# Sixteen weight units: VectorE makes all low parts of the projections' weights, GpSimd none

## The chip, the cores and the metric

One Trainium2 chip, one core. The metric is device time in microseconds (us) of one execution. TensorE ran at its full granted clock (1.00) in the profiled execution.

## What is computed

One layer of a streaming encoder over 576 tokens (512 of a prompt, 64 new ones with a cache of 128 rows), in float32. In short:

```
h   = x @ W_in                       # columns: k, q, v of two head groups, an index part, forget gates
mix = concat(ForgettingAttention(h_A),      # 8 heads: scores + decay, causal mask, softmax, @ V
             IndexedSparseAttention(h_B))   # 8 heads: rope, only the top-k rows by an index score
x   = LN1(alpha * x + mix @ W_o)
x   = LN2(alpha * x + relu(x @ W_up)^2 @ W_down)
x   = x + sigmoid(x @ W_g + b_g) * (p @ W_ple)
```

The top-k is 128 of up to 512 rows for the prompt, 48 of 192 for the sample. The part of the program that matters here is the projection to k, q and v and the attention that runs beside it.

## The kernel before, in words

Every large product is made in three passes of TensorE: a float32 operand is split into a high part and a low part (the rest), and high x high, high x low and low x high are summed. For a weight this takes three steps. A DMA on SP's queue brings the raw unit `wraw` (128 x 1024). ScalarE rounds it into the high half of `whl` (line 149, CAST). Then `raw - high` gives the low half (line 155, TENSOR_TENSOR). For the 24 units of the k, q and v projections each step is cut into two pieces of 128 x 512, so two high pieces and two low pieces per unit. Which engine makes the low pieces is the argument `eng` of `Weights.split`: VectorE (DVE), or GpSimd (POOL) when a unit was added with `pool_l`. In the kernel before, units 0 to 7 (k, q, v of head pairs 0 and 1, k and q of pair 2) have their low pieces on VectorE and units 8 to 23 (v of pair 2 up to v of pair 7) on GpSimd. The output projection's units and all later ones are on VectorE.

`WT.step()` is called after every six matmuls and emits one piece if its data have been asked for long enough ago and a `whl` buffer is free. There are three `whl` and three `wraw` buffers in this part. Two units are thus prepared ahead of the one in use.

The projections are a loop over head pairs p = 0 to 7. In it `drive(proj(p + 1), 24, ticks(9), 27)` interleaves the 24 steps of the next pair's three projections with 27 steps of the attention of pair p. A pair has nine attention jobs (4 query blocks x 2 heads for the prompt, one for the sample). A job goes through the engines in a row of stages:

- `qk` (TensorE, lines 890 to 900): scores into a PSUM buffer `S`;
- `addmax` (VectorE, line 908): adds the bias and finds the row maximum, `S` to `sP`;
- `exp` (ScalarE, line 913), then `norm`: a reciprocal (VectorE, line 918) and a multiply, on ScalarE for pairs 0 to 3 and for the sample (line 920), on VectorE for the others (line 922);
- `ptrans` (TensorE, line 56): transposes `sP` into a PSUM buffer `T`; `pevac` (line 953) copies it to `PT`;
- after the last job `pv` (TensorE, lines 966 to 975) multiplies by V, and `oevac` (lines 985, 986) splits the result.

`S`, `T` and `X` share three PSUM buffers, so a late `addmax` or `pevac` stops TensorE.

Beside it run, on VectorE, the top-k selection (`choice`, lines 708 and 710: eight maxima of a row, then eight replaced, 16 times per block; it ends in pair 4) and, for pairs 4 to 7, the rotary embedding of k and q (lines 788 to 797: ScalarE copies four pieces `xr`, VectorE does three passes over 128 x 576). GpSimd also makes the low part of k (`KLP`, lines 810 and 811, two of 64 x 512 for each of the pairs 2 to 7).

The order on each engine is the program's order as a scheduler lays it out when the kernel is built. Each engine then works through its own list in order and waits where an input is not there.

Of the kernel before, what the change touches and what calls it, by code (L numbers as in the profile page):

```python
# [36 lines left out]
def tile_hybrid_step(ctx: ExitStack, tc: tile.TileContext, I, O):  # L37
# [241 lines left out]
    WT = Weights()  # L279
# [94 lines left out]
    U = {}  # L374
    WT.ring(sbw, 3, 3, "a")
    qkv = I["w_qkv"]
    for p in range(8):
        for x, kind in enumerate("kqv"):
            U[kind, p] = WT.add(qkv[p * 3 + x], 128, pool_l=(p * 3 + x > 7))
    for j in range(8):  # L380
        U["o", j] = WT.add(I["w_o6"][j], 128)
    for k in (6, 7):
# [1463 lines left out]
```

## Time and profile before

| | |
|---|---|
| median of 3 runs | 765.42 us (765.17 to 766.64) |
| the profiled execution: its time, its span | 766.22 us, 764.5 us |
| TensorE matmuls busy | 751.9 us (98%) |
| VectorE busy | 571.8 us (75%), 1119 instructions |
| ScalarE busy | 472.8 us (62%) |
| GpSimd busy | 109.8 us (14%), 130 instructions |
| GpSimd on line 155 | 42.2 us, 32 instructions, from 78.2 to 228 us of the span |
| DMA | 101.35 MB, 133 GB/s in the mean |

Busy time of TensorE is counted up to the modelled end of each matmul, so 98% busy does not mean that it ran at its peak. The chain of waits is followed back from the last instruction; idle time of an engine that nothing waits for costs nothing. In the rows of the timeline the columns are: start, duration, engine, line, operation, output <- input, shape and count, and in brackets the idle time before it with what ended it.

### The profile page before, as it was taken

How to read it: one execution, taken by the hardware profiler on the slowest of the kernel's cores; microseconds unless marked ns; L12 is line 12 of the kernel's file. 1: busy time of each engine (PE TensorE's matmuls, PEld its weight loads, DVE VectorE, ACT ScalarE, POOL GpSimd, SP SyncE). 2: the span in 40 equal slices, each digit the busy share in tenths (PEclk: the TensorE clock that was granted, in tenths of full speed). 3: DMA queues.
4: the chain of work that ended last, by engine and by line, in shares of the span. 5: the costliest groups of instructions: out<-in, count | busy, mean ns of one | idle time of the engine just before them, and what ended most of it. 6: DMA issues, size and time to landing. Idle time of an engine off the chain costs nothing.

```text
span 764.5 us, 14624 instructions
## 1 busy us (share of the span) xinstructions
PE 751.9 (98%) x5679; PEld 731.5 (96%) x5679; DVE 571.8 (75%) x1119; ACT 472.8 (62%) x931; POOL 109.8 (14%) x130
## 2 busy tenths in 40 slices
PE   9999999999999999999999999999999999999997
PEld 7999988999899999999999999999999999999997
DVE  6788888888777865779777579866898666657643
ACT  6589777897676635788654577435764466625451
POOL 7100324344241000100000000000000000011000
PEclk9999999999999999999999999999999999999999
DMA  8438344244222315352546666667667664730001
GB/s 288 167 70 150 128 134 122 93 139 176 78 85 86 114 58 173 111 177 80 123 110 176 148 159 172 148 164 180 155 149 178 152 154 152 288 111 30 28 29 69
DMA packets 38197, 101.35 MB, mean 133 GB/s; under 512 B 6000, under 2 KB 10224, under 8 KB 38000
## 3 DMA queue, kind: packets, MB, share of 16 engines
q1 hardware_dynamic: 34384, 87.61, 37.1%
q0 software_dynamic: 3456, 12.58, 10.1%
q8 instruction: 44, 0.72, 0.4%
q10 hardware_dynamic: 288, 0.22, 0.1%
q14 instruction: 25, 0.20, 0.1%
HBM read 85.26 MB, written 9.54 MB: 124 GB/s over the span
## 4 chain that ended last, share of the span: by engine, by line
PE 80%; DVE 12%; ACT 6%; issue 2%; DVEq 0%; ACTq 0%
PE g L305 39%; PE m L305 15%; PE n L305 13%; PE g L293 2%; PE T L56 2%; PE V L975 2%; DVE dbias L710 2%; DVE whl L155 1%; ACT xr L788 1%; DVE m L708 1%; ACT whl L149 1%; PE m L469 1%; PE m L483 1%; PE S L900 1%; PE S L898 1%
## 5 line engine op out<-in xcount | busy, mean ns | idle before, releaser
L149 ACT CAST whl<-wraw 128x1024 fp32r<-128x1024 f32 (+2 forms) x190 | 154.9, 828 | 83.9 <-PE g L305 50.0
L155 DVE TENSOR_TENSOR whl<-wraw,whl 128x1024 fp32r<-128x1024 f32 (+2 forms) x158 | 157.8, 1008 | 53.4 <-ACT whl L149 52.8
L305 PE MATMUL m<-AH,whl 128*128 128x288 f32 x736 | 176.7, 307 | 0.0
L305 PE MATMUL g<-BH,whl 128*128 128x288 f32 (+2 forms) x680 | 143.3, 298 | 0.0
L305 PEld LDWEIGHTS m<-AH,whl 128*128 128x128 f32 x736 | 126.4, 188 | 1.7 <-issue 1.0
L305 PEld LDWEIGHTS g<-BH,whl 128*128 128x128 f32 x680 | 111.1, 188 | 1.3
L305 PE MATMUL m<-AL,whl 128*128 128x288 f32 x368 | 108.8, 296 | 0.0
L305 PE MATMUL g<-BL,whl 128*128 128x288 f32 (+2 forms) x340 | 100.6, 296 | 0.3 <-DVE BL L1250 0.3
L305 PEld LDWEIGHTS m<-AL,whl 128*128 128x128 f32 x368 | 69.5, 189 | 0.6
L305 PEld LDWEIGHTS g<-BL,whl 128*128 128x128 f32 x340 | 64.0, 188 | 0.9 <-DVE BL L1250 0.7
L210 POOL DMA_DIRECT2D wraw<-in_w_dram x24 | 20.8, 866 | 287.1 <-DMA wraw<-in_w_dram 207.5
L913 ACT ACTIVATE sP<-sP,st 128x128 f32<-128x128 f32 (+4 forms) x72 | 39.4, 549 | 35.4 <-DVE st L908 35.3
L155 POOL TENSOR_TENSOR whl<-wraw,whl 128x512 fp32r<-128x512 f32 x32 | 42.2, 1334 | 90.1 <-ACT whl L149 74.9
L305 PE MATMUL m<-BH,whl 128*128 128x288 f32 x192 | 43.0, 302 | 0.0
L305 PE MATMUL g<-s,whl 128*128 128x288 f32 x288 | 42.1, 295 | 0.0
L305 PE MATMUL n<-BH,whl 128*128 128x288 f32 x192 | 42.0, 294 | 0.0
L305 PEld LDWEIGHTS g<-s,whl 128*128 128x128 f32 x288 | 39.5, 188 | 0.0
L56 PE MATMUL T<-ident,sP 128*128 128x128 f32 (+1 forms) x176 | 31.3, 273 | 1.5 <-DVE sP L922 0.6
L305 PEld LDWEIGHTS m<-BH,whl 128*128 128x128 f32 x192 | 32.0, 188 | 0.5 <-issue 0.3
L305 PEld LDWEIGHTS n<-BH,whl 128*128 128x128 f32 x192 | 32.0, 188 | 0.0
L1520 ACT ACTIVATE g<-n 128x288 f32<-128x288 f32 x24 | 9.5, 395 | 35.6 <-PE n L305 35.6
L305 PE MATMUL m<-BL,whl 128*128 128x288 f32 x96 | 28.3, 294 | 0.0
(331 smaller groups left out, 1664.3 us busy)
## 6 DMA issues: line engine op xcount, KB each, us to landing
wraw<-in_w_dram SPq DMA_DIRECT2D x48, 512.0 KB, 4.0
wraw<-in_w_dram POOLq DMA_DIRECT2D x24, 512.0 KB, 5.8
wraw<-in_w_qkv_dram SPq DMA_DIRECT2D x23, 512.0 KB, 3.7
wraw<-in_w_dram SPq DMA_DIRECT2D x24, 256.0 KB, 4.3
wraw<-in_w_up_dram SPq DMA_DIRECT2D x8, 512.0 KB, 3.9
wraw<-in_w_down_dram SPq DMA_DIRECT2D x8, 512.0 KB, 4.1
wraw<-in_w_gate_dram SPq DMA_DIRECT2D x8, 512.0 KB, 4.2
wraw<-in_w_o_dram SPq DMA_DIRECT2D x8, 384.0 KB, 3.0
```

What stands on the lines that cost most here:

```text
L56: PE.transpose(out, in_, ident[:n, :n])
L149: ACT.copy(self.hv[u][:, 0, c], src["tile"][:, c])
L155: eng.tensor_tensor(t[:, 1, c], src["tile"][:, c], f(t[:, 0, c]), OP.subtract)
L210: POOL.dma_start(t[:, :n], it["acc"], accum_op=OP.add)
L293: PE.matmul(ps, W(w, k, slice(0, 128)), a[:, k, sl], start=(len(terms) == 2 and n == 0), stop=False)
L305: mm = PE.matmul(ps, W(w, kw, wc), a[:, ka, cols], start=(first and i == 0), stop=(last and i == n - 1), skip_group_check=more)
L469: PE.matmul(mk[:, h, :HW], w0(part, k), a[:, k, h * HW:(h + 1) * HW], start=(k == 0 and i == 0), stop=(k == 7 and i == 2))
L483: PE.matmul(acc[b][:n[b], :304], a[:, k, b * 128:b * 128 + n[b]], ixw(part, k), start=(k == 0 and i == 0), stop=(k == 7 and i == 2))
L710: tc.keep_in_program_order(DVE.match_replace(out=s, in_to_replace=m, in_values=s, imm_value=GONE))
L913: ACT.activation(j["P"], j["P"], AF.Exp, bias=j["st"][:, 0:1], scale=-1.0, accum_out=j["st"][:, 2:3])
L975: PE.matmul(ps[r, x * 256 + c.start:x * 256 + c.stop], P["vt"][:, kb, r], t[:, hh, kb, c], start=(kb == 0), stop=(kb == n - 1))
L1520: ACT.mul(P.e, P.o, -1.0)
```

## The change

The argument `pool_l` is dropped for the 24 units, so `Weights.split` gets VectorE for all of them.

```diff
     for p in range(8):
         for x, kind in enumerate("kqv"):
-            U[kind, p] = WT.add(qkv[p * 3 + x], 128, pool_l=(p * 3 + x > 7))
+            U[kind, p] = WT.add(qkv[p * 3 + x], 128)
```

32 instructions of 128 x 512 leave GpSimd's list and stand in VectorE's. The scheduler lays out VectorE's list anew around them; ScalarE's changes at some places with it, and TensorE's at one (three matmuls of a projection move ahead of two transposes).

The first place is on VectorE in the attention of pair 2, where the top-k selection of block 2 (`dbias2`) runs beside the additions for the softmax (`sP_...<-S_...,causal`). Before:

```order
L708 MAX m8_118<-dbias2_111 128x8
L710 MATCH_REPLACE dbias2_111<-m8_118,dbias2_111 128x384
L708 MAX m8_118<-dbias2_111 128x8
L908 ISA sP_1625,st_1626<-S_1604,causal_113 128x128
L908 ISA st_1626 128x1
L710 MATCH_REPLACE dbias2_111<-m8_118,dbias2_111 128x384
L918 RECIPROCAL st_1586<-st_1586 128x1
L708 MAX m8_118<-dbias2_111 128x8
L918 RECIPROCAL st_1626<-st_1626 128x1
L710 MATCH_REPLACE dbias2_111<-m8_118,dbias2_111 128x384
```

In the changed kernel, from the same MAX on:

```order
L708 MAX m8_118<-dbias2_111 128x8
L155 TENSOR_TENSOR whl_1600<-wraw_1241,whl_1600 128x512
L710 MATCH_REPLACE dbias2_111<-m8_118,dbias2_111 128x384
L908 ISA sP_1625,st_1626<-S_1604,causal_113 128x128
L908 ISA st_1626 128x1
L708 MAX m8_118<-dbias2_111 128x8
L918 RECIPROCAL st_1586<-st_1586 128x1
L155 TENSOR_TENSOR whl_1600<-wraw_1241,whl_1600 128x512
L710 MATCH_REPLACE dbias2_111<-m8_118,dbias2_111 128x384
L918 RECIPROCAL st_1626<-st_1626 128x1
```

The two low pieces of a unit stand between the steps of the selection, and the selection's steps have moved back against the softmax: the MATCH_REPLACE and MAX behind the first MAX are now behind it by a softmax addition. A little further, before the first addition of 128 x 256 columns of this pair, 11 MAX and 11 MATCH_REPLACE of `dbias2` stood, and 11 and 10 stand now.

The second place is on VectorE in pair 3, where q of pair 4 is rotated (lines 789 to 791) while the jobs `sP_2256` (384 columns) and `sP_2288` (the sample's, bias `biasS`) are at their softmax. Before:

```order
L908 ISA sP_2256,st_2257<-S_2238,causal_113 128x384
L908 ISA st_2257 128x1
L908 ISA sP_2288,st_2289<-S_2275,biasS_114 128x192
L908 ISA st_2289 128x1
L789 SCALAR_TENSOR_TENSOR x32_2244<-m_2103,cosT_105 128x576
L790 TENSOR_TENSOR xr_2245<-xr_2245,sinT_106 128x576
L918 RECIPROCAL st_2257<-st_2257 128x1
L791 TENSOR_TENSOR x32_2244<-x32_2244,xr_2245 128x576
L918 RECIPROCAL st_2289<-st_2289 128x1
L908 ISA sP_2331,st_2332<-S_2315,causal_113 128x512
```

In the changed kernel:

```order
L908 ISA sP_2256,st_2257<-S_2238,causal_113 128x384
L908 ISA st_2257 128x1
L155 TENSOR_TENSOR whl_2271<-wraw_1940,whl_2271 128x512
L789 SCALAR_TENSOR_TENSOR x32_2244<-m_2103,cosT_105 128x576
L790 TENSOR_TENSOR xr_2245<-xr_2245,sinT_106 128x576
L908 ISA sP_2288,st_2289<-S_2275,biasS_114 128x192
L908 ISA st_2289 128x1
L791 TENSOR_TENSOR x32_2244<-x32_2244,xr_2245 128x576
L918 RECIPROCAL st_2257<-st_2257 128x1
L155 TENSOR_TENSOR whl_2271<-wraw_1940,whl_2271 128x512
L908 ISA sP_2331,st_2332<-S_2315,causal_113 128x512
```

The sample's addition now stands behind the low piece and two of the three passes of the rotation, and its reciprocal (not shown, it follows lines 796, 797 and a MATCH_REPLACE) behind the next job's addition.

The third place is ScalarE's list at the same moment. Before:

```order
L913 ACTIVATE sP_2256,st_2257<-sP_2256,st_2257 128x384
L913 ACTIVATE sP_2288,st_2289<-sP_2288,st_2289 128x192
L920 ACTIVATE sP_2256<-sP_2256,st_2257 128x384
L953 COPY PT_2318<-T_2299 128x3x128
L794 CAST qE_2242<-x32_2244 64x576
L795 CAST qO_2243<-x32_2244 64x576
L799 COPY QS0_166<-x32_2244 64x64 x2
L920 ACTIVATE sP_2288<-sP_2288,st_2289 128x192
```

In the changed kernel:

```order
L913 ACTIVATE sP_2256,st_2257<-sP_2256,st_2257 128x384
L953 COPY PT_2318<-T_2299 128x3x128
L913 ACTIVATE sP_2288,st_2289<-sP_2288,st_2289 128x192
L794 CAST qE_2242<-x32_2244 64x576
L920 ACTIVATE sP_2256<-sP_2256,st_2257 128x384
L795 CAST qO_2243<-x32_2244 64x576
L799 COPY QS0_166<-x32_2244 64x64 x2
L913 ACTIVATE sP_2331,st_2332<-sP_2331,st_2332 128x512
L953 COPY PT_2318<-T_2343 128x3x128
L747 COPY v32_2360<-m_2246 128x576
L920 ACTIVATE sP_2288<-sP_2288,st_2289 128x192
```

Both multiplies of line 920, which release transposes on TensorE, have moved back: the one of 384 columns behind line 794, the sample's behind the next job's exponential, a copy and line 747. In pairs 4 and 5 the sample's addition and its multiply move in the same way.

## Prediction, made before the changed kernel ran

> **What bounds the kernel now.** First the page, then the stretch of the change, then who stops TensorE in it.
>
> ```profile
> span 764.5 us, 14624 instructions
> PE 751.9 (98%) x5679; PEld 731.5 (96%) x5679; DVE 571.8 (75%) x1119; ACT 472.8 (62%) x931; POOL 109.8 (14%) x130
> L155 POOL TENSOR_TENSOR whl<-wraw,whl 128x512 fp32r<-128x512 f32 x32 | 42.2, 1334 | 90.1 <-ACT whl L149 74.9
> ```
>
> TensorE is busy for all but 12.6 us of the span. So the time moves only as far as TensorE's waits move. The third row is what the change takes from GpSimd: 32 x 1.334 = 42.2 us, all between 78 and 228 us. GpSimd waits ahead of them (90.1 us), and TensorE waits for none of them. The stretch as a whole, with columns length, PE, PEld, DVE, ACT and POOL busy (instructions), TensorE clock, DMA share and GB/s:
>
> ```profile
> core 0: us, PE busy (x) PEld busy (x) DVE busy (x) ACT busy (x) POOL busy (x), PEclk, DMA share, GB/s
> 78.00:230.00 152.00, 148.50 (x1175) 140.53 (x1174) 125.31 (x376) 116.76 (x291) 58.07 (x46) 1.00 0.38 118
> ...
> 110.00:120.00 10.00, 8.98 (x75) 8.35 (x76) 9.72 (x36) 7.97 (x21) 3.93 (x4) 1.00 0.33 112
> ```
>
> VectorE is busy for 125.31 of 152 us (82%) and idle for 26.7. TensorE idles 3.5 us. The fullest ten microseconds of VectorE, 110 to 120, are also those in which TensorE idles most (1.02 us). The waits of TensorE from 60 to 265 us, in us, times and longest:
>
> ```profile
> PE X L966 <- DVE st L908: 0.9, 1, 0.9
> PE T L56 <- DVE sP L922: 0.6, 1, 0.6
> PE S L890 <- ACT cosT L676: 0.6, 1, 0.6
> PE S L898 <- DVE st L908: 0.3, 1, 0.3
> PE X L56 <- ACT v L747: 0.3, 1, 0.3
> PE T L56 <- ACT sinT L676: 0.2, 1, 0.2
> PE T L56 <- ACT sP L920: 0.2, 1, 0.2
> PE T L56 <- DVE st L908: 0.2, 1, 0.2
> PE X L56 <- DVE st L908: 0.2, 1, 0.2
> ```
>
> They are 3.5 us together. That caps what the change can gain. All wait for the softmax chain on VectorE and ScalarE or for a copy; none waits for a weight. The loss has no such cap: a late addition or reciprocal on VectorE stops TensorE directly.
>
> **What leaves, what comes.** The 42.2 us on GpSimd were on no path, so taking them away gains nothing by itself. The low piece on VectorE is shown where it is made there already:
>
> ```profile
> 71.34 0.69 DVE L155 TENSOR_TENSOR whl<-wraw,whl 128x512 fp32r<-128x512 f32 x1
> 71.95 0.75 DVE L774 SCALAR_TENSOR_TENSOR qs<-m,qs 128x576 fp32r<-128x576 f32 x1
> ```
>
> It takes 0.69 us, and the next instruction starts 0.61 us after it. 32 of them take 32 x 0.61 = 19.5 us of VectorE's time.
>
> Against this stands what GpSimd's pieces cost VectorE. Two of their 16 pairs, the passes that VectorE ran beside them, and the groups of one pass inside and behind the stretch:
>
> ```profile
> 98.13 2.52 POOL L155 TENSOR_TENSOR whl<-wraw,whl 128x512 fp32r<-128x512 f32 x2 [6.00 <-ACT whl L149]
> 99.55 1.32 DVE L683 SCALAR_TENSOR_TENSOR dbiasS<-cosT,iw,dbiasS 64x192 f32<-64x192 f32 x1
> ...
> 218.90 1.41 DVE L791 TENSOR_TENSOR x<-x,xr 128x576 f32<-128x576 f32 x1
> L790 DVE TENSOR_TENSOR xr<-xr,sinT 128x576 f32<-128x576 f32 x6 | 7.4, 1235 | 0.0
> L790 DVE TENSOR_TENSOR xr<-xr,sinT 128x576 f32<-128x576 f32 x2 | 1.5, 748 | 0.0
> ```
>
> The pass of line 790 takes 0.75 us behind 230 us, where GpSimd makes no low pieces, and 1.235 in the mean inside. The pass at 99.55 ends at 100.87, just behind GpSimd's pair (98.13 + 2.52 = 100.65), and took 1.32 us where its like takes 0.41 (the row at 102.00 below). Eight passes of VectorE, the first at 99.55 and the last at 218.90, sit in this way behind a low piece. Their surplus over the free price is 0.91, 1.10, 0.83, 0.91, 0.66, 0.63, 0.91 and 0.66, together 6.6 us. So VectorE gets 19.5 - 6.6 = 12.9 us more to do, against 26.7 us idle. It would be busy for about 138 of 152 us (91%).
>
> The Trainium skill's Perfetto Trace Analysis, section Optimizing Scalar/DVE Operations, speaks against the change: where VectorE is saturated, work may well be handed to ScalarE or even GpSimd. Read strictly, all 12.9 us would be path and the median 778.3. The same sentence adds that between these two engines it might not help, since they share a port, and the 6.6 us agree with that half.
>
> The low pieces themselves are not due soon. Two units are prepared ahead of the one in use, no wait for `whl` stands in the list above, and GpSimd took 1.334 us for a piece that VectorE makes in 0.69. So a piece may stand a few instructions later in a list and delays nothing. The DMA that refills `wraw` waits for the same piece and is covered by the same distance; SP's queue gets nothing new. GpSimd's pieces of k, which stood behind its low pieces, can only start earlier.
>
> **Stretch a, 98 to 120 us.**
>
> ```profile
> 102.00 0.41 DVE L683 SCALAR_TENSOR_TENSOR dbiasS<-sinT,iw,dbiasS 64x192 f32<-64x192 f32 x1 [0.80 <-ACT sinT L676]
> L710 DVE MATCH_REPLACE8 dbias<-m,dbias 128x384 f32<-128x384 f32 x16 | 8.7, 542 | 0.0
> 118.83 0.41 DVE L908 CUSTOM_DVE_ANT_0 sP<-S,causal 128x256 f32<-128x256 f32 x1
> 119.31 0.34 PE L966 MATMUL X<-PTs,Vc 128*64 128x64 f32 x4 [0.88 <-DVE st L908]
> ```
>
> From 102.00 VectorE works without a gap until the addition at 118.83, and TensorE waits 0.88 us for it. By the new order two low pieces come in ahead of that addition and one MATCH_REPLACE of 0.54 (0.62 with the loading of its values) goes behind it. A piece that stands between a MAX and the MATCH_REPLACE that needs it also covers about 0.1 us between them, so two cost about 1.0: +0.4. At the start the 0.91 of the pass at 99.55 goes; the pieces that replace it run mostly in the 0.9 us in which VectorE waited before 99.06. VectorE and ScalarE are then about 0.65 us earlier at 102.00, and TensorE's 0.2 us there goes. Net: **-0.25 us**.
>
> **Stretch b, 157 to 167 us**, where the order moves the sample's job most:
>
> ```profile
> 157.94 0.36 DVE L908 CUSTOM_DVE_ANT_0 sP<-S,biasS 128x192 f32<-128x192 f32 x1 [1.12 <-PE S L891]
> 159.67 0.76 DVE L789 SCALAR_TENSOR_TENSOR x<-m,cosT 128x576 f32<-128x576 f32 x1 [1.37 <-ACT xr L788]
> 161.28 1.58 DVE L791 TENSOR_TENSOR x<-x,xr 128x576 f32<-128x576 f32 x1
> 158.35 0.62 ACT L149 CAST whl<-wraw 128x512 fp32r<-128x512 f32 x1
> 161.07 0.45 ACT L913 ACTIVATE sP<-sP,st 128x192 f32<-128x192 f32 x1
> 161.50 0.61 ACT L920 ACTIVATE sP<-sP,st 128x384 f32<-128x384 f32 x1
> 162.89 0.67 ACT L794 CAST qE<-x 64x576 fp32r<-64x576 f32 x1 [0.41 <-DVE x L791]
> 164.81 0.45 ACT L920 ACTIVATE sP<-sP,st 128x192 f32<-128x192 f32 x1
> 166.23 0.64 ACT L747 COPY v<-m 128x576 f32<-128x576 f32 x1
> 162.55 0.49 PE L56 MATMUL T<-ident,sP 128*128 128x128 f32 x3
> 165.31 0.44 PE L56 MATMUL T<-ident,sP 128*128 128x128 f32 x2 [0.22 <-ACT sP L920]
> ```
>
> The first low piece waits for ScalarE's high one (158.35 + 0.62 = 158.97) and runs to 159.6, inside the 1.37 us before 159.67: hidden. But the sample's addition waits in the list behind it and behind lines 789 and 790, so it runs at 161.0 instead of 157.94. The pass of 791 follows without its 0.83 and ends at 162.1. ScalarE: exponential of the sample to 161.9, line 794 to 162.8, and only then the multiply of 384 columns, to 163.4. Its transposes stood at 162.55: TensorE waits 0.9. The sample's multiply now follows lines 795 (like 794, 0.67) and 799, an exponential, a copy and line 747. Before, 799 began at 164.2 (two of 0.67 behind 162.89) and line 747 ended at 166.87, with the sample's multiply (0.36 to the next start) among them: 2.3 us without it. So it ends near 163.4 + 0.67 + 2.3 + 0.4 = 166.75, or a little before where ScalarE waited among them; I take 166.65. Its transposes stood at 165.31, now 166.0 (0.9 later, without their 0.22): another 0.65. Sum: 0.9 + 0.65 - 0.22 = **+1.35 us**. TensorE being later, its next two waits for line 908 (0.2 and 0.3 us above) go: **-0.5**.
>
> **The rest.** From 177 to 186 us the last steps of the selection and the second piece press on the multiplies of 256 columns on VectorE: between nothing and 0.9 (the size of b's first wait), I take +0.3, since VectorE's 0.91 at line 790 goes there too. From 187 to 196 the waits of 0.6 and 0.2 us have the same form as b, but line 922 is on VectorE, and the 0.66 of line 791 goes while a piece of 0.61 comes: -0.35, half of them, as TensorE arrives later by then. In pair 5 (215 to 224 us) the same walk ends before TensorE needs the transposes: 0. Behind 230 us nothing changes. Sum: -0.25 + 1.35 - 0.5 + 0.3 - 0.35 = **+0.55 us**.
>
> The profiled execution (766.22 us, of which 1.72 lie around the span) stands 0.80 above the median. On the profile the sum gives 766.8, on the median 765.42 + 0.55 = **766.0 us**.
>
> **Rivals.** *VectorE's lists run full* (slower). If the 12.9 us are not spread into the idle time but meet the softmax chain in each of pairs 3, 4 and 5 as in b, two more b's come (+2.7), and the +0.3 becomes 0.9: 769.3. For it: 91% in the mean, and the ten microseconds from 110 already at 97%. Against it: the new order moves the selection, which nothing waits for before pair 4's last jobs, back behind the additions.
>
> *The waits go* (faster). The walks in b and behind it rest on tenths of a microsecond. If the 6.6 us of blocked passes is what holds the softmax chain, the waits for VectorE (0.9, 0.6, 0.3, 0.2, 0.2) go and b does not come: 765.4 - 2.2 = 763.2. It decides this if the multiply of 384 columns in b ends before 162.55. Against it: ScalarE's list there stands as shown.
>
> *The low pieces are themselves blocked by GpSimd's k pieces* (slower). These stay on GpSimd, and pair 7 shows the meeting:
>
> ```profile
> 237.79 0.54 DVE L155 TENSOR_TENSOR whl<-wraw,whl 128x384 fp32r<-128x384 f32 x1
> 238.24 1.38 DVE L922 TENSOR_SCALAR sP<-sP,st 128x256 f32<-128x256 f32 x1
> 237.99 1.49 POOL L810 TENSOR_TENSOR KLP<-x,kE 64x512 fp32r<-64x512 f32 x1 [9.95 <-PE m L305]
> ```
>
> The multiply of 256 columns waits about 1.0 us for line 810. A low piece in its place at pairs 2 to 6 could lose as much five times. In pair 7 TensorE did not wait; if two of the five meet the path, with b: 766.0 + 2.0 = 768.0.
>
> The Trainium skill's SBUF — State Buffer, section Who interferes with whom, calls the port that VectorE and GpSimd share an exclusive lock. The 1.38 us agree. By that rule alone the change would swap one lock for another.
>
> **How the numbers follow.** 0.2% (1.5 us) is about what a measurement of this kernel can tell from no change. Chances: my sum within 1.5 us of the median 0.58, lists run full 0.19, low pieces blocked 0.10, waits go 0.13. Same 0.58; slower 0.29; faster 0.13. The likeliest case alone spans 764.4 to 766.9. The range takes in most of the two slower cases and the edge of the faster one: 763.8 to 769.0.
>
> **What would show it.** Right: line 155 with 32 more on VectorE at about 0.69 us and none on GpSimd; lines 790 and 791 at 0.75 in the stretch; VectorE at 138 us there; a wait of `T L56` for `sP L920` in pair 3; TensorE's waits up by about half a microsecond. Wrong: additions of line 908 that start over 3 us behind their scores in several pairs, or low pieces well above 0.7 us.

## The result, and the profile after

The changed kernel takes 770.11 us (median; 770.08 to 770.39), the kernel before 765.46 beside it. The ratio is 1.006, 95% interval 1.0048 to 1.0073: slower by 4.65 us, and outside the predicted range of 763.8 to 769.0. The profiled execution took 770.1 us, its span 768.4.

The page of the changed kernel: busy time of the engines, and the group of line 155 on VectorE (before: 158 instructions, 157.8 us).

```profile
PE 752.0 (98%) x5679; PEld 730.5 (95%) x5679; DVE 586.2 (76%) x1151; ACT 473.5 (62%) x931; POOL 68.7 (9%) x98
L155 DVE TENSOR_TENSOR whl<-wraw,whl 128x1024 fp32r<-128x1024 f32 (+2 forms) x190 | 182.7, 970 | 58.0 <-ACT whl L149 57.2
```

TensorE does the same 752 us of work, so the loss is waiting. The stretch of the prediction (columns as there), and then three groups of VectorE from 60 to 230 us:

```profile
78.00:230.00 152.00, 145.44 (x1147) 136.91 (x1146) 137.47 (x403) 116.35 (x286) 16.61 (x14) 1.00 0.38 117
```

```profile
L155 DVE TENSOR_TENSOR whl<-wraw,whl 128x512 fp32r<-128x512 f32 x35 | 26.9, 772 | 4.9 <-ACT whl L149 4.8
L791 DVE TENSOR_TENSOR x<-x,xr 128x576 f32<-128x576 f32 x6 | 4.7, 776 | 0.0
L790 DVE TENSOR_TENSOR xr<-xr,sinT 128x576 f32<-128x576 f32 x6 | 4.5, 749 | 0.0
```

VectorE is busy for 137.47 us, as forecast (138), and lines 790 and 791 run nearly free (0.749 and 0.776 us). The same work now ends later, though: from 77.6 to 233.5 us, where it stands in this trace, VectorE is busy for 140.1 us. And a low piece takes 0.772 us in the mean instead of 0.69. TensorE's waits from 60 to 269 us:

```profile
PE T L56 <- ACT sP L920: 3.2, 5, 1.0
PE X L966 <- DVE st L908: 1.4, 1, 1.4
PE T L56 <- DVE sP L922: 1.0, 2, 0.6
PE S L890 <- ACT cosT L676: 0.6, 1, 0.6
PE X L56 <- ACT v L747: 0.3, 1, 0.3
```

They are 6.5 us instead of 3.5: the transposes of softmax rows (`T L56`) wait 4.2 us, before 0.8 for the same two lines.

Where the time went is seen best by matching TensorE's instructions of the two traces in their order and taking the difference of their start times. This table is worked out in that way from the two timelines (set to 0 at 70 us; places are times of before; us). It has a row for every kernel that is told of below. In the names, "changed" and "before" are the kernel that the edit starts from, "back" means on GpSimd again, "alone" means that only these units moved to VectorE, and "k pieces" are lines 810 and 811.

| at | 104 | 124 | 150 | 160 | 181 | 186 | 198 | 228 | 270 |
|---|---|---|---|---|---|---|---|---|---|
| changed | -0.38 | -0.49 | 0.11 | 0.56 | 1.55 | 2.62 | 3.18 | 3.62 | 3.62 |
| changed, small k pieces | -0.46 | -0.59 | -0.59 | -0.59 | -0.01 | -0.05 | -0.07 | 0.38 | -0.05 |
| changed, k units back | -0.47 | -0.58 | -0.58 | -0.58 | 0.14 | 0.11 | -0.20 | 0.26 | 0.23 |
| changed, unit 18 back | -0.36 | -0.47 | 0.13 | 0.59 | 1.57 | 1.54 | 1.24 | 1.68 | 1.69 |
| changed, q units back | -0.38 | -0.51 | 0.09 | 0.56 | 1.46 | 2.46 | 2.48 | 2.46 | 2.45 |
| changed, q pieces later | -0.36 | -0.48 | 0.11 | 0.58 | 1.48 | 2.56 | 1.98 | 1.68 | 1.66 |
| before, q units alone | 0.00 | 0.00 | -0.01 | -0.01 | 0.52 | 0.48 | 0.19 | 0.67 | 0.67 |
| before, k units alone | 0.35 | 0.34 | 0.61 | 0.61 | 0.61 | 2.44 | 2.46 | 2.43 | 2.41 |
| before, unit 18 alone | 0.01 | 0.00 | 0.00 | 0.00 | -0.01 | 1.84 | 1.85 | 1.85 | 1.86 |
| before, v units alone | -0.02 | 0.32 | 0.32 | 0.32 | 0.96 | 0.92 | 0.02 | 0.03 | 0.02 |
| before, v units and pair 7's k pieces | 0.00 | 0.33 | 0.33 | 0.34 | 0.99 | 0.96 | 0.07 | 0.09 | -0.32 |
| changed, all k pieces on VectorE | 0.17 | 0.05 | 1.23 | 2.30 | 2.13 | 1.88 | 1.74 | 2.17 | 1.75 |
| before, small k pieces | 0.00 | 0.01 | 0.01 | 0.00 | -0.35 | -0.39 | -0.35 | -0.39 | -0.82 |

In the row of the changed kernel 3.62 us are lost by 228 us, in jumps. The largest between two columns is 1.07 us, from 181 to 186. The rest of the spans' difference (3.9 us) lies at the two ends, and the profiled execution of before stood 0.76 above its median of 765.46. So about 1 us of the 4.65 by the medians is not located here.

That jump in the traces, first before (VectorE's pass of line 790 and its multiply, GpSimd's low piece of k, TensorE's transposes):

```profile
179.41 1.66 DVE L790 TENSOR_TENSOR xr<-xr,sinT 128x576 f32<-128x576 f32 x1
182.57 0.35 DVE L922 TENSOR_SCALAR sP<-sP,st 128x256 f32<-128x256 f32 x1
182.84 0.69 DVE L708 MAX8 m<-dbias 128x8 f32<-128x512 f32 x1
182.65 1.43 POOL L810 TENSOR_TENSOR KLP<-x,kE 64x512 fp32r<-64x512 f32 x1 [2.20 <-ACT kE L805]
183.52 0.38 PE L56 MATMUL T<-ident,sP 128*128 128x128 f32 x2
```

and then in the changed kernel:

```profile
182.12 0.68 DVE L710 MATCH_REPLACE8 dbias<-m,dbias 128x512 f32<-128x512 f32 x1
182.78 1.43 DVE L155 TENSOR_TENSOR whl<-wraw,whl 128x512 fp32r<-128x512 f32 x1
184.13 1.36 DVE L922 TENSOR_SCALAR sP<-sP,st 128x256 f32<-128x256 f32 x1
182.38 1.28 POOL L810 TENSOR_TENSOR KLP<-x,kE 64x512 fp32r<-64x512 f32 x1 [15.38 <-ACT kE L805]
183.73 1.62 POOL L811 TENSOR_TENSOR KLP<-x,kO 64x512 fp32r<-64x512 f32 x1
185.64 0.41 PE L56 MATMUL T<-ident,sP 128*128 128x128 f32 x2 [0.56 <-DVE sP L922]
```

Before, the multiply started 0.08 us ahead of line 810 and took 0.35. Now a low piece that starts inside line 810 takes 1.43 us, ending half a microsecond behind it, and the multiply behind it falls into line 811 and takes 1.36. Where 0.35 us stood on VectorE, 2.8 stand, and TensorE waits. Free, the two would take about 1.0 (0.69 and 0.35). The new order has also put a step of the selection (182.12) ahead of the multiply. A pass is called held here where it takes longer beside an instruction of GpSimd than the same pass without one. The theories for the experiments were: **K**, VectorE's passes are held by GpSimd's lines 810 and 811; **P**, the place of the q units' pieces ahead of the sample's softmax (the stretch b of the prediction); **L**, VectorE's load, so much for each piece.

### The profile page after: what moved, and what is told of

The parts are those of the page before. It is cut to its first block, busy times and chain, and to the rows that moved or that the text cites. A ratio compares the mean times of both kernels' runs of the same rounds, so it can differ in the third digit from the quotient of the medians.

```text
span 768.4 us, 14614 instructions
## 1 busy us (share of the span) xinstructions
PE 752.0 (98%) x5679; PEld 730.5 (95%) x5679; DVE 586.2 (76%) x1151; ACT 473.5 (62%) x931; POOL 68.7 (9%) x98
## 4 chain that ended last, share of the span: by engine, by line
PE 75%; DVE 15%; ACT 8%; issue 1%; DMA 1%; DVEq 0%; ACTq 0%
PE g L305 38%; PE n L305 13%; PE m L305 12%; DVE whl L155 3%; PE g L293 2%; ACT xr L788 2%; DVE dbias L710 2%; PE T L56 2%; DVE m L708 2%; ACT whl L149 1%; PE V L975 1%; DVE sP L908 1%; PE m L469 1%; PE m L483 1%; DVE dbias L683 1%
## 5 line engine op out<-in xcount | busy, mean ns | idle before, releaser
L155 DVE TENSOR_TENSOR whl<-wraw,whl 128x1024 fp32r<-128x1024 f32 (+2 forms) x190 | 182.7, 970 | 58.0 <-ACT whl L149 57.2
L56 PE MATMUL T<-ident,sP 128*128 128x128 f32 (+1 forms) x176 | 31.5, 275 | 4.5 <-ACT sP L920 3.2
L56 PEld LDWEIGHTS T<-ident,sP 128*128 128x128 f32 (+1 forms) x176 | 21.6, 138 | 7.1 <-ACT sP L920 4.4
```

The source lines that it names most:

```text
L56: PE.transpose(out, in_, ident[:n, :n])
L155: eng.tensor_tensor(t[:, 1, c], src["tile"][:, c], f(t[:, 0, c]), OP.subtract)
```

## The experiments

The kernel before was timed beside them and took 765.77 to 765.90 us, 0.3 to 0.4 more than beside the changed kernel, which was timed in the first session alone. So a difference from 770.11 us carries that much doubt, and the ratios are to the kernel before. Units are numbered k, q, v from pair 0 on, so 9, 12, 15, 18, 21 are k units, 10, 13, 16, 19, 22 q units.

**Three q units back on GpSimd.**

```diff
-            U[kind, p] = WT.add(qkv[p * 3 + x], 128)
+            U[kind, p] = WT.add(qkv[p * 3 + x], 128, pool_l=(p * 3 + x in (16, 19, 22)))
```

> As the changed kernel, but the six low pieces of the q units of pairs 5, 6 and 7 (units 16, 19, 22) are on GpSimd again; 26 pieces stay moved. Theory P (place): the loss sits where these three units' pieces stand, ahead of the sample's addition and the rotation of q; in the changed kernel TensorE waits there 1.04 + 0.72 (pair 3), 0.43 + 0.68 (pair 4) and 0.52 us (pair 5), 3.4 us together, so 770.1 falls to about 766.7. Theory L (load): VectorE has 19.5 us more to do and every piece costs the same share of the 4.65 us lost, 0.145 us; 26 pieces give 765.5 + 3.8 = 769.2. Theory K (lock): the loss comes from GpSimd's pieces of k (lines 810, 811), which hold up VectorE; they are untouched, so 770.

768.89 us, ratio 1.004 (1.0028 to 1.0053). Only 1.2 us came back; P is not the main cause. Near L's number, but in the table the loss comes in the same jumps as in the changed kernel up to 186 us, not evenly.

**Only these q units on VectorE.**

```diff
+            U[kind, p] = WT.add(qkv[p * 3 + x], 128, pool_l=(p * 3 + x > 7 and p * 3 + x not in (16, 19, 22)))
```

> As the kernel before, but the six low pieces of units 16, 19 and 22 alone are on VectorE. Theory P: nearly the whole loss, 765.5 + 3.4 = 768.9. Theory L: 6 of 32 pieces, 765.5 + 0.9 = 766.3. Theory K: almost nothing, 765.5, since the units whose pieces meet lines 810 and 811 are the others.

766.70 us, ratio 1.001 (1.0001 to 1.0019). The two waits of stretch b come with these three units alone, and a third in pair 5:

```profile
163.48 0.55 PE L56 MATMUL T<-ident,sP 128*128 128x128 f32 x3 [0.97 <-ACT sP L920]
166.79 0.44 PE L56 MATMUL T<-ident,sP 128*128 128x128 f32 x2 [0.71 <-ACT sP L920]
...
224.00 0.44 PE L56 MATMUL T<-ident,sP 128*128 128x128 f32 x2 [0.55 <-ACT sP L920]
```

P's waits are real, but 1.7 us of waiting in pair 3 costs 0.5 by 181 us, since TensorE, once late, waits less for what follows. The kernel loses 0.9 us in all by P (766.70 against 765.83).

**The q units' pieces held back behind the rotation** (all on VectorE). Their low pieces are due 8 steps after the high ones instead of 2, and are emitted behind the last pass of the rotation.

```diff
-                        lo_at[0] = clock[0] + 2
+                        lo_at[0] = clock[0] + (8 if u in (16, 19, 22) else 2)
...
+                    with tc.issue_after(rotated[0]) if u in (16, 19, 22) else ExitStack():
```

> All 32 pieces on VectorE as in the changed kernel, but the pieces of units 16, 19 and 22 are emitted six steps later and held in VectorE's list behind the last pass of the rotation of q (line 797 of the kernel before). The load on VectorE is the same, only the place of six pieces differs; the sample's addition and both multiplies of ScalarE are back in their old order. Theory P: 766.7 as in the experiment that gives these pieces back to GpSimd. Theory L and theory K: 770.

767.80 us, ratio 1.0027 (1.0017 to 1.0037). In pair 3 nothing was gained: the two waits became 0.61 us (for the copy to `PTs`) at 169 and 0.78 at 171, and the table has 1.48 at 181 us, like the 1.55 of the changed kernel. The gain lies in pairs 4 and 5: behind 186 us this row wins 0.9 where the changed kernel loses 1.0. There P had 1.63 of its 3.4 us; L and K had nothing.

**Small pieces of k.** Lines 810 and 811 of pairs 2 to 7 do 64 of their 512 columns (the rest of k's low parts is left out); the lists of the other engines stay as in the changed kernel.

```diff
-        q(lambda: eng.tensor_tensor(KL[lo, 0], k32[lo, :NP], f(QE[lo, :NP]), OP.subtract))
+        q(lambda n=64 if p > 1 else NP: eng.tensor_tensor(KL[lo, 0, :n], k32[lo, :n], f(QE[lo, :n]), OP.subtract))
...
```

> As the changed kernel, but GpSimd's pieces of k for pairs 2 to 7 (lines 810, 811) work on 64 of 512 columns, so most of the low part of k is left out for these pairs. The lists of VectorE, ScalarE and TensorE are the same as in the changed kernel, row for row; GpSimd holds VectorE up for about 0.3 us at a time and not 1.3. Theory K: TensorE's wait of 0.56 us for line 922 in pair 4 goes, and up to 1 us each at pairs 2, 3, 5: 768 to 769. Theories P and L: 770.

766.23 us, ratio 1.0006 (0.9997 to 1.0014): less than even K expected. All low pieces are on VectorE, each in its place in the list, and 3.9 of the 4.65 us are gone. The same pass and multiply as above:

```profile
180.71 0.67 DVE L155 TENSOR_TENSOR whl<-wraw,whl 128x512 fp32r<-128x512 f32 x1
181.30 0.41 DVE L922 TENSOR_SCALAR sP<-sP,st 128x256 f32<-128x256 f32 x1
180.31 0.31 POOL L810 TENSOR_TENSOR KLP<-x,kE 64x64 fp32r<-64x64 f32 x1 [15.38 <-ACT kE L805]
181.00 0.57 POOL L811 TENSOR_TENSOR KLP<-x,kO 64x64 fp32r<-64x64 f32 x1 [0.38 <-ACT kO L806]
```

L falls with it as the main cause: the load is what it was in the changed kernel but for the held time.

**The same edit on the kernel before.** This tells whether short lines 810 and 811 gain by themselves.

> The kernel before with lines 810 and 811 of pairs 2 to 7 done on 64 of their 512 columns (the rest of the low parts is left out), as in the run of the changed kernel with small pieces, which gained 3.9 us. Theory K: before, few of VectorE's passes met these lines (from 227 to 241 us, 2.4 us held in all, and 0.5 at 164), so there is little to gain: 764.8 to 765.8 us. Rival M (shorter lines 810 and 811 free TensorE or another engine whatever VectorE does): about 3.9 us off here too, 762 us.

765.16 us, ratio 0.9993 (0.9985 to 1.0002). By the medians 0.6 us are gained, against 3.9 in the changed kernel; the table has 0.82, of which 0.35 lie between 160 and 181 us and 0.43 behind 228, at pair 7's pieces. So most of the cost belongs to the meeting of the change with lines 810 and 811. Not all of it: with small k pieces on both sides the change still costs 1.1 us by the medians (766.23 against 765.16) and 0.8 in the table, about what the q units cost alone. The expectation misread the trace of before: lines 810 and 811 held VectorE's multiply for 0.48 us at 184.77 and 1.02 at 210.95 as well as in pair 7, while the 0.5 at 164 and part of the 2.4 stand beside other lines. The table shows nothing gained at those two places, so they were on no path.

**The k units back on GpSimd.**

```diff
+            U[kind, p] = WT.add(qkv[p * 3 + x], 128, pool_l=(p * 3 + x in (9, 12, 15, 18, 21)))
```

> The low pieces of five units (the k units of pairs 3 to 7, numbers 9, 12, 15, 18 and 21, whose pieces stand around lines 810 and 811) go back to GpSimd; the eleven others stay on VectorE. Theory K (VectorE's low pieces and softmax multiplies are held by GpSimd's lines 810 and 811): the blocked passes of line 155 at 89.6, 119.1, 153.1 and 182.8 us go, and what is left is the 0.9 us that the q units cost alone: 766.7 to 767.5 us. Rival V (the v units' pieces, which the run of the q units alone also left on GpSimd, carry the other 3 us): 769 to 770 us. Rival L (load): eleven of sixteen units, 768.8 us.

766.52 us, ratio 1.0009 (1.0 to 1.0018). Eleven of sixteen units are on VectorE and 3.6 of the 4.65 us are gone. That is K's way and just below its range.

**Only the k units on VectorE.**

```diff
+            U[kind, p] = WT.add(qkv[p * 3 + x], 128, pool_l=(p * 3 + x > 7 and x > 0))
```

> Of the sixteen units only the k units of pairs 2 to 7 (numbers 9, 12, 15, 18 and 21) have their low pieces on VectorE; q and v units stay on GpSimd as before. Theory K: the loss of 3 us that is neither the q units' nor the load's comes with these five units: 768 to 769 us, with blocked passes of line 155 beside lines 810 and 811. Rival V: as before, 765.8 to 766.3 us. Rival L: 767.3 us.

768.34 us, ratio 1.0034 (1.0021 to 1.0046). K again. In the table 1.83 us of its 2.41 fall between 181 and 186 us, which is one unit's pieces.

**Only unit 18, the k unit of pair 6, on VectorE.** Two instructions change engine; TensorE's list is that of before, VectorE's and ScalarE's are laid out anew around them.

```diff
+            U[kind, p] = WT.add(qkv[p * 3 + x], 128, pool_l=(p * 3 + x > 7 and p * 3 + x != 18))
```

> The kernel before with one unit of the sixteen on VectorE, number 18 (the k unit of pair 6, its two pieces at 182 us); TensorE's list is that of before. Theory K: its second piece is held by line 810, the multiply of line 922 behind it by line 811, and TensorE's transposes wait for that multiply: the interval from 177 to 206 us goes from 29.0 to 30.6 to 30.9 us as in the run of the k units alone, 767.4 to 767.7 us. Rival S (the k units' cost is spread over the five, 0.5 us each): 766.3 us. Rival L: 766.0 us.

767.75 us, ratio 1.0025 (1.0015 to 1.0035). One unit of the sixteen costs 1.85 us:

```profile
179.02 0.75 DVE L790 TENSOR_TENSOR xr<-xr,sinT 128x576 f32<-128x576 f32 x1
181.82 1.37 DVE L155 TENSOR_TENSOR whl<-wraw,whl 128x512 fp32r<-128x512 f32 x1
183.11 1.35 DVE L922 TENSOR_SCALAR sP<-sP,st 128x256 f32<-128x256 f32 x1
181.36 1.28 POOL L810 TENSOR_TENSOR KLP<-x,kE 64x512 fp32r<-64x512 f32 x1 [11.07 <-ACT kE L805]
182.71 1.61 POOL L811 TENSOR_TENSOR KLP<-x,kO 64x512 fp32r<-64x512 f32 x1
184.61 0.41 PE L56 MATMUL T<-ident,sP 128*128 128x128 f32 x2 [1.33 <-DVE sP L922]
```

Line 810 starts 1.3 us earlier than at 182.65 before, of which 0.4 is the two executions' offset. The other 0.9 is the surplus that left line 790: with GpSimd's pieces away from 177.86 to 180.46, line 790 runs free (0.75 us at 179.02, 1.66 before), k is finished earlier, and line 810 comes forward, onto the low piece and the multiply. No run holds line 810 at its old time; had it started there, the low piece would have run ahead of it and only the multiply would have met it (an estimate from these rows).

**The changed kernel with only unit 18 back.**

```diff
+            U[kind, p] = WT.add(qkv[p * 3 + x], 128, pool_l=(p * 3 + x == 18))
```

> The changed kernel with this one unit, number 18, on GpSimd again; the fifteen others stay on VectorE. Theory K: the interval from 177 to 206 us goes from 30.6 us back to 28.7 us, and nothing else changes: 768.1 us. Rival S: 769.6 us. Rival L: 769.8 us.

767.97 us, ratio 1.0027 (1.0017 to 1.0037). The complement agrees: 2.14 us come back. In the table the jump from 181 to 186 is gone and the next one (186 to 198) turns from +0.56 to -0.30; up to 181 us and behind 198 the rows move alike.

**Lines 810 and 811 of all pairs on VectorE as well**, all low pieces there.

```diff
-        eng = POOL if p > 1 else DVE
+        eng = DVE
```

> The changed kernel with lines 810 and 811 of pairs 2 to 7 on VectorE as well: twelve passes more of 0.67 to 0.69 us each (8.2 us), and nothing on GpSimd that can hold VectorE in these stretches. Theory K: the hold goes, the passes stand where VectorE had to wait anyway: 766 to 767.5 us. Rival L (VectorE's load delays its lists): 8.2 us more load on top of 19.5 at the same price of 0.24 us for each us: 772 us.

767.58 us, ratio 1.0024 (1.0014 to 1.0033), just above K's 766 to 767.5. 8.2 us more load than the changed kernel and 2.5 us faster. It isn't free either: the table has 2.3 us lost by 160 us. TensorE waits 0.8 and 1.2 us for line 920 in pair 3, and 1.2 us for the cosine of line 676 at 100 us.

**Only the v units on VectorE**, and **the same with pair 7's lines 810 and 811 there too**: a version meant to beat both kernels.

```diff
+            U[kind, p] = WT.add(qkv[p * 3 + x], 128, pool_l=(p * 3 + x > 7 and x < 2))
...
-        eng = POOL if p > 1 else DVE
+        eng = POOL if 1 < p < 7 else DVE
```

> Of the sixteen units only the v units (numbers 8, 11, 14, 17, 20 and 23) have their low pieces on VectorE; k and q units stay on GpSimd. Read off the intervals between the products of the pairs in the earlier runs: the first (88 to 119 us) is 0.5 us shorter in every run in which the v units were on VectorE, the fourth (177 to 206 us) 0.3 us shorter in the run of the q and v units, and nothing else hangs on them. Theory K: 765.0 us, the first of these kernels below the kernel before. Rival L (load, six of sixteen units at the same price): 767.4 us.

> As the run of the v units alone, and lines 810 and 811 of pair 7 on VectorE. Theory K: the two multiplies of line 922 that these lines held in every kernel with full pieces (1.03 and 0.71 us at 238 to 240 us before) run free, and the interval from 234 to 264 us goes from 30.7 to 30.3 us, as it did in all three runs without these pieces on GpSimd: 764.6 us. Rival: the two passes of 0.68 us stand in VectorE's list ahead of the same multiplies and cost what the hold cost: 765.0 us.

765.93 us, ratio 1.0 (0.9991 to 1.0009), and 765.54, ratio 0.9996 (0.9987 to 1.0006). The first expectation was wrong. The 0.5 us in the first interval that I had ascribed to the v units does not come with them alone (the table has -0.02 at 104 and +0.32 at 124), and what they lose in pair 3 (0.64) they win back in pair 4 (0.93). The second edit did what K said: 0.41 us at pair 7's pieces, where the multiplies of line 922 run in 0.35 us beside line 810's old place.

```profile
237.50 0.54 DVE L155 TENSOR_TENSOR whl<-wraw,whl 128x384 fp32r<-128x384 f32 x1
237.96 0.35 DVE L922 TENSOR_SCALAR sP<-sP,st 128x256 f32<-128x256 f32 x1
238.42 0.68 DVE L810 TENSOR_TENSOR KLP<-x,kE 64x512 fp32r<-64x512 f32 x1
...
240.52 0.35 DVE L922 TENSOR_SCALAR sP<-sP,st 128x256 f32<-128x256 f32 x1
```

That is below what a measurement of this kernel can tell, so no version here is shown to beat the kernel before.

## Why the prediction was wrong, point by point

- **Load: right.** 32 more passes of line 155 on VectorE, lines 790 and 791 nearly free, 137.47 us busy against 138 forecast (140.1 over the same work, with the held time in it). The rival *lists run full* is refuted as the main cause: with the same lists and small k pieces 3.9 of the 4.65 us are gone. Its price, 769.3, lay nearest to the result, but that is a number and not its mechanism; it also lay above the range's end of 769.0, which was said to take in most of the slower cases.
- **Stretch a: right in kind.** -0.25 forecast, -0.49 at 124 us, and TensorE's wait of 0.2 us there is gone, as forecast. One reading was wrong without harm: two of TensorE's listed waits, 0.8 us together, are for line 676, the index part's activation, and not for the softmax or a copy.
- **Stretch b and its credit: right.** The walk gave waits of 0.9 and 0.65 us, the trace 1.04 and 0.72, by the way described: line 794 goes ahead of the multiply of 384 columns, and the sample's multiply stands behind line 747.

```profile
163.28 0.67 ACT L794 CAST qE<-x 64x576 fp32r<-64x576 f32 x1 [0.23 <-DVE x L791]
163.86 0.61 ACT L920 ACTIVATE sP<-sP,st 128x384 f32<-128x384 f32 x1
167.33 1.07 ACT L920 ACTIVATE sP<-sP,st 128x192 f32<-128x192 f32 x2
...
164.52 0.55 PE L56 MATMUL T<-ident,sP 128*128 128x128 f32 x3 [1.04 <-ACT sP L920]
167.84 0.33 PE L56 MATMUL T<-ident,sP 128*128 128x128 f32 x1 [0.72 <-ACT sP L920]
```

  From 160 to 181 us the sum was +1.35 - 0.5 = +0.85; the table has 1.55 - 0.56 = 0.99.
- **177 to 186 us, "+0.3, between nothing and 0.9": the step that failed most.** Measured 1.07, outside its own bounds, and 1.85 with unit 18 alone. The step named "the second piece" that presses on the multiplies, but the piece had only its free price of 0.61 us, the multiply itself got nothing, and the bound of 0.9 was taken from another stretch. Held by lines 810 and 811, the two took 2.8 us. The sign that the prediction had set for being wrong, "low pieces well above 0.7 us", came with it.
- **187 to 196 us, -0.35, and pair 5, 0:** measured +0.56 (186 to 198) and +0.44. Pair 5's has the form of stretch b (the wait of 0.55 at 224 us in the run of the q units alone); the walk there had ended "before TensorE needs the transposes". The +0.56 turns into -0.30, near the forecast, when unit 18 goes back, and into +0.02 when the q units go back. So it takes both the jump ahead of it and the q units' pieces.
- **No term for 124 to 160 us:** +1.05, gone with small k pieces and with the k units back. Held pieces stand there or just ahead (119.06 us with a surplus of 1.04, 153.06 with 0.49), but the steps from them to TensorE are waits of under 0.3 us each and were not followed one by one, so the path of this part stays open.
- **The rival that held.** "The low pieces are themselves blocked by GpSimd's k pieces" had the mechanism, a chance of 0.10 and 768.0 us. Its price was too low in two ways: a held piece counted 1.0 us and the pass behind it nothing, though the row of pair 7 it was read from is just such a pass, a multiply of the softmax; and two meetings on the path were counted where four units' pieces were held (the rows below and the one at 182.78), each with softmax work close behind it. The sentence that GpSimd's pieces of k "can only start earlier" was put down as harmless, and the rows of unit 18 alone speak for it as part of the harm.

```profile
89.59 1.52 DVE L155 TENSOR_TENSOR whl<-wraw,whl 128x512 fp32r<-128x512 f32 x1
119.06 1.72 DVE L155 TENSOR_TENSOR whl<-wraw,whl 128x512 fp32r<-128x512 f32 x1
153.06 1.18 DVE L155 TENSOR_TENSOR whl<-wraw,whl 128x512 fp32r<-128x512 f32 x1
```

Stretch by stretch (to 124, 160, 181, 186, 198 and 228 us) the forecast was -0.25, 0, +0.85, +0.3, -0.35 and 0, together +0.55; the table has -0.49, +1.05, +0.99, +1.07, +0.56 and +0.44, together 3.62.

By the runs: of the 3.62 us in the changed kernel's row, 3.4 go when the k units go back (3.62 - 0.23), and the three q units alone make 0.67. The parts do not simply add: alone, the k, the three q and the v units make 2.41, 0.67 and 0.02, together 3.1. The medians agree with the two larger parts (3.6 of 4.65 us, and 0.9).

## What to carry to other kernels

When work moves from GpSimd to VectorE, list which VectorE passes fall beside the GpSimd work that stays, in the new order and at the new times: a pass moved in front of a released one can double the hold, because the next pass then meets GpSimd's next instruction. The sum of held time says little (by passes that took over 0.35 us more than free, VectorE lost about 11 us from 60 to 265 us before and 7 after the change); what counts is whether a pass that TensorE waits for is among the held ones. A test that changes two lines is to shrink the GpSimd instructions and leave every list as it is, on both kernels, since what it gains on the kernel before has to be taken off.

## What the runs showed of the hardware

Not every pass of VectorE is held beside GpSimd. In the eleven traces without small k pieces and with low pieces of the weights or of k on GpSimd, passes of 60 to 270 us that start inside lines 155, 810 or 811 of GpSimd took, in the median against the free one: line 155 1.44 us against 0.68, line 791 1.42 against 0.75, line 922 with 256 columns 1.36 against 0.35. The selection's MAX8 (0.69 with 512 columns), MATCH_REPLACE8 (0.68), the addition of line 908 (0.54 with 384), line 789 (0.76) and the copy of line 953 (0.28) took what they take free. The MAX8 in the first fence of the jump, beside line 810, is one of them.

The held ones read both inputs from SBUF, or are the multiply of line 922; lines 789, 908 and 953 read one input from PSUM, and MAX8 has one input. MATCH_REPLACE8's row names two, but the eight values of `m` come in by an instruction of their own in front of it (MATCH_VALUE_LOAD, 0.08 us). The Trainium skill's SBUF — State Buffer, section Who interferes with whom, says that a VectorE instruction with two SBUF inputs contends with a GpSimd instruction that reads SBUF, that `tensor_scalar` can contend in a two-port mode, and that one with a single SBUF input outside such modes does not. The traces agree in every group above.

It also says, of the two-port modes, that whoever issues first gets the shared ports for the whole instruction. The trace agrees: the multiply that started 0.08 us ahead of line 810 took its free 0.35 us, and line 810 then took 1.43 us instead of 1.28. With VectorE's pass between lines 810 and 811, line 811 takes 1.62 instead of 1.28 to 1.30, so GpSimd waits too.
